# The first half of the down projection moved between the units of the up projection, as seven products throughout

## The chip, the cores and the metric

The kernel runs on one core of a Trainium2 chip. The metric is device time in microseconds (us) of one launch: the median of three runs before the change is 1566.11 us (1565.74 to 1566.63). The engines are named as the profile names them: PE (TensorE; its weight loads are PEld), DVE (VectorE), ACT (ScalarE), POOL (GpSimd) and SP (SyncE, which issues most DMAs).

## The reference

One block of a streaming encoder on 256 tokens, width 2048: a retention branch and a latent-attention branch are merged and added to the residual, and then comes the part that this case is about:

```python
h = h + mixer(rmsnorm(h))                      # all that comes before
z = rmsnorm(h, norm_mlp_g) @ w_up              # 256 x 2048 @ 2048 x 8192
h = h + square(relu(z)) @ w_down               # 256 x 8192 @ 8192 x 2048
return rmsnorm(h, norm_f_g)
```

Everything is float32. The row scale of the second rmsnorm is a positive number per token, so the kernel leaves it out of `z` and multiplies the down projection's result with its square (`rh2`).

## The kernel before

**Precision.** Each float32 operand is split in two fp32r parts: hi, a cast on ACT (`split`, L550), and lo, the difference, on DVE (L551). A product is then three matmuls: hi times hi, hi times lo, lo times hi.

**Three ways to multiply.** All take 256 tokens.
- A *unit* (`Unit`, L1239) makes 128 columns of `z`, transposed (columns on the partitions), with the weight as the stationary operand: 16 matmuls of 512 columns (L176: hi and lo of the tokens side by side) and 16 of 256 (L180), in two parts of 8 and 8, each with its own 512 KB load. Its result stands in one PSUM bank. `evict` (L1263) copies it on ACT (L1266), adds the two halves on DVE (L1267), and a little later Relu and Square on ACT and a store to DRAM (`hid`) follow.
- An *Eight* (`Eight`, L380) multiplies 256 rows by 1024 columns the plain way: a 2 by 2 product of blocks, 8 block products of 3 matmuls, 24 of 512 columns, in two parts. Tokens are the stationary operand. It sums in four banks, roles 0, 1, 4 and 7.
- A *seven-product step* (`Step` L287, `Seven` L417) does the same block product with 7 block products, 21 matmuls, in four parts of 6, 6, 6 and 3. It needs combinations of the weights, made on DVE (`prep`: fa at L307, fb at L316 and L317), and of the tokens (four mixed matrices), and seven banks, whose sums are combined at the end (`s_end` or `partial`). Its weight parts are 3.5 splits of 1024 columns.

**Up projection.** 8192 columns are 64 tiles of 128. The first 24 tiles are three blocks of 1024 columns, each 8 seven-product steps over the 2048 rows; the other 40 are units, set between the parts of the steps (after part 1 or part 3). The steps take mixed matrices of the normalised tokens, made by `hc.make` (L252). A step block's result has tokens on the partitions, so it is combined into `zo` (`s_end`, L515) and turned by 16 PE transposes per block (`turn`, L1277, L1284).

**Down projection.** `half` 0 gives the first 1024 output columns, half 1 the others; each runs over 32 pairs of hidden tiles. Half 0 has 10 Sevens and 22 Eights, half 1 12 Sevens and 20 Eights (`DS`). Each pair is loaded from `hid` and split again in both halves (`Hidden`, L1335); for a Seven its four mixed matrices are made once (`mix`, L1347, and `cut`), kept in `comb` and used again in half 1. The seven-products of a half are combined by `partial` (L444) some parts after its last Seven, into `gt[:, 1]`, and added to the residual `hn2` by `fold` (L1385) and `finish` (L1389). In half 0 the four roles stand in the pool `pmm` (4 banks) and the three other products in `pat` (4 banks); in half 1 it is the other way around (`Banks.add`, L349).

**Order.** The order of the work on each engine is written out by hand (`manual_schedule`): `stream` (L470) goes through a list of parts. Before a part's matmuls it issues the loads up to six parts ahead and the splits up to four parts ahead (`AHEAD`); after them come evictions, and then what stands in the list `later`, each entry after so many parts. Every engine's queue is in this order. Split parts stand in a ring of seven (`pair`), raw weights in five and two (`raw`, `sraw`). The residual (2 MB, POOL's queue) and `norm_f_g` (1 MB) are loaded at the first parts of half 0 (L1472 to L1476).

Of the kernel before, what the change touches and what calls it, by code (L numbers as in the profile page):

```python
# [30 lines left out]
SU = 3  # L31
SJ = KT // 2
ST = SU * 1024 // P
EARLY, LATE = 3, 2
AHEAD = 4
PAIRED = 6
MAKE = 7, 2 * EARLY + 18
SUMS = (4, 7, 10), (0, 1, 2)
# [7 lines left out]
DS = (4, 7, 9, 12, 14, 17, 19, 22, 24, 27), (3, 5, 7, 9, 11, 13, 15, 17, 19, 21, 24, 27)  # L46
# [59 lines left out]
def block_kernel(ctx: ExitStack, tc: tile.TileContext, A):  # L106
# [138 lines left out]
    class Combos:  # L245
        FORM = {2: 0, 5: 1, 6: 2, 4: 3}
        RAW = {1: (1, 0), 3: (0, 1), 7: (1, 1)}

        def __init__(self, name, pair):
            self.name, self.pair, self.t = name, pair, []  # L250

        def make(self, c):  # L252
            if c % 2 == 0:
                self.t.append(big(f"{self.name}{c // 2}", F32R, (P, KT // 4, 2, 4, P)))
            return combine(self.pair, 2 * c, self.t[-1][:, c % 2 * 2 : c % 2 * 2 + 2])

        def get(self, f, j):
            if f in self.RAW:
                k, t = self.RAW[f]
                ts = slice(t * P, (t + 1) * P)  # L260
                return self.pair.hi(2 * j + k, ts), self.pair.lo(2 * j + k, ts)
            o = self.t[j // 4][:, j % 4]
            return o[:, 0, self.FORM[f]], o[:, 1, self.FORM[f]]

# [22 lines left out]
    class Step:  # L287
        def __init__(self, qs, src, x, j, between, end):
            self.qs, self.src, self.x, self.j, self.between, self.end = qs, src, x, j, between, end
            self.ws = {}  # L290

        def load(self, part):
            if part:
                return
            self.rb = wtile("raw", [P, 2, 512])
# [9 lines left out]
        def prep(self, part):  # L305
            if part == 0:
                V.tensor_tensor(  # L307
                    out=self.fa, in0=self.rb[:, 1:].to_broadcast([P, 2, 512]), in1=self.ra, op=ALU.add
                )
                self.middle()  # L310
# [8 lines left out]
        def middle(self):  # L319
            pass  # L320

        def mm(self, part):
            if part == 0 and self.j == 0:
                self.qs.update({f: (mmps if f in (3, 4, 2, 5) else atps)(f"zs{uid[0]}{f}") for f in (3, 4, 2, 5, 6, 1, 7)})
            if part == 1:
                self.between()
# [90 lines left out]
    class Seven(Step):  # L417
# [4 lines left out]
        def load(self, part):  # L422
            if part == 0:
                self.h.load()
# [1166 lines left out]
```

## Time and profile before

| | |
|---|---|
| median of 3 runs | 1566.11 us (1565.74 to 1566.63) |
| span of the profiled execution | 1564.8 us |
| its own time beyond the span | not in the profile; the runs' median is 1.3 us above its span |
| PE busy | 1551.3 us (99%), 7655 matmuls |
| DVE busy | 1316.0 us (84%) |
| ACT busy | 962.6 us (62%) |
| POOL busy | 39.3 us (3%) |
| HBM | 319.72 MB read, 12.58 MB written, 212 GB/s over the span |

The page gives busy time per engine for the whole span; a window row gives the same for one stretch. In a timeline row stand the start in us from the span's first instruction, the duration, engine, line, operation, output<-inputs, shapes, and, in brackets, the idle time ahead of it with what ended it. A row with "x8" merges eight instructions. PE's matmuls overlap: the distance from start to start is what one costs, not the duration.

### The profile page before, as it was taken

How to read it: one execution, taken by the hardware profiler on the slowest of the kernel's cores; microseconds unless marked ns; L12 is line 12 of the kernel's file. 1: busy time of each engine (PE TensorE's matmuls, PEld its weight loads, DVE VectorE, ACT ScalarE, POOL GpSimd, SP SyncE). 2: the span in 40 equal slices, each digit the busy share in tenths (PEclk: the TensorE clock that was granted, in tenths of full speed). 3: DMA queues.
4: the chain of work that ended last, by engine and by line, in shares of the span. 5: the costliest groups of instructions: out<-in, count | busy, mean ns of one | idle time of the engine just before them, and what ended most of it. 6: DMA issues, size and time to landing. Idle time of an engine off the chain costs nothing.

```text
span 1564.8 us, 21391 instructions
## 1 busy us (share of the span) xinstructions
PE 1551.3 (99%) x7655; PEld 1311.0 (84%) x7655; DVE 1316.0 (84%) x1787; ACT 962.6 (62%) x1416; POOL 39.3 (3%) x76
## 2 busy tenths in 40 slices
PE   9999999999999999999999999999999999999997
PEld 7888888888898888888888888888888888888886
DVE  7898877799976988976567689887978899989996
ACT  6645655566545667875445567676767766656664
POOL 0000000000000000000000000000000100000000
PEclk9999999999999999999999999999999999999999
DMA  9666755566656654444556657666675977686873
GB/s 319 207 203 208 230 164 161 159 201 206 206 168 220 213 197 143 157 136 161 185 206 211 236 196 247 214 226 232 207 249 188 376 265 245 237 304 211 266 255 115
DMA packets 107626, 333.70 MB, mean 213 GB/s; under 512 B 11264, under 2 KB 12160, under 8 KB 106496
## 3 DMA queue, kind: packets, MB, share of 16 engines
q1 hardware_dynamic: 104208, 318.71, 61.1%
q0 software_dynamic: 3168, 11.54, 1.9%
q10 hardware_dynamic: 144, 2.10, 0.4%
q8 instruction: 60, 0.98, 0.3%
q14 instruction: 46, 0.38, 0.1%
HBM read 319.72 MB, written 12.58 MB: 212 GB/s over the span
## 4 chain that ended last, share of the span: by engine, by line
PE 79%; DVE 1%; issue 1%; ACT 1%; DVEq 0%; POOLq 0%; POOL 0%; ACTq 0%
PE z L176 9%; PE dn L358 7%; PE dn L359 7%; PE dn L357 7%; PE z L180 5%; PE zs L333 2%; PE zs L334 2%; PE zs L335 2%; PE mo L214 2%; PE mo L215 2%; PE mo L217 2%; PE wo L214 2%; PE wo L215 2%; PE wo L217 2%; PE gm L357 2%; PE yr L358 2%
## 5 line engine op out<-in xcount | busy, mean ns | idle before, releaser
L551 DVE TENSOR_TENSOR lo<-raw,hi 128x1024 fp32r<-128x1024 f32 (+3 forms) x214 | 232.0, 1101 | 22.7 <-ACT hi L550 22.2
L169 DVE TENSOR_TENSOR lo<-raw,hi 128x1024 fp32r<-128x1024 f32 (+1 forms) x148 | 173.2, 1171 | 89.7 <-ACT hi L168 89.6
L168 ACT CAST hi<-raw 128x1024 fp32r<-128x1024 f32 (+1 forms) x148 | 149.6, 1011 | 155.9 <-PE mo L215 44.9
L550 ACT CAST hi<-raw 128x1024 fp32r<-128x1024 f32 (+3 forms) x214 | 200.0, 953 | 55.3 <-issue 9.5
L551 DVE TENSOR_TENSOR morelo<-raw,morehi 128x1024 fp32r<-128x1024 f32 (+1 forms) x118 | 127.1, 1098 | 18.8 <-ACT morehi L550 18.3
L550 ACT CAST morehi<-raw 128x1024 fp32r<-128x1024 f32 (+1 forms) x118 | 109.1, 949 | 10.5 <-issue 3.2
L550 ACT CAST hi<-forms 128x1024 fp32r<-128x1024 f32 x70 | 73.7, 1052 | 51.2 <-DVE forms L307 28.1
L176 PE MATMUL z<-hT,morehi 128*128 128x512 f32 x408 | 101.6, 391 | 0.0
L357 PE MATMUL dn<-hi,dd 128*128 128x512 f32 x230 | 89.6, 389 | 0.0
L359 PE MATMUL dn<-hi,dd 128*128 128x512 f32 x230 | 89.5, 389 | 0.0
L358 PE MATMUL dn<-lo,dd 128*128 128x512 f32 x230 | 89.5, 389 | 0.0
L551 DVE TENSOR_TENSOR lo<-forms,hi 128x1024 fp32r<-128x1024 f32 x70 | 85.0, 1221 | 5.3 <-ACT hi L550 4.9
L176 PEld LDWEIGHTS z<-hT,morehi 128*128 128x128 f32 x408 | 74.9, 188 | 14.4
L1266 ACT COPY hs<-z 128x512 f32<-128x512 f32 x40 | 23.5, 587 | 71.2 <-PE z L180 71.1
L357 PE MATMUL dn<-morehi,dd 128*128 128x512 f32 x156 | 60.7, 389 | 0.0
L358 PE MATMUL dn<-morelo,dd 128*128 128x512 f32 x156 | 60.7, 389 | 0.0
L359 PE MATMUL dn<-morehi,dd 128*128 128x512 f32 x156 | 60.7, 389 | 0.0
L180 PEld LDWEIGHTS z<-hT,morelo 128*128 128x128 f32 x408 | 55.6, 190 | 4.0
L176 PE MATMUL z<-hT,hi 128*128 128x512 f32 x232 | 57.9, 392 | 0.0
L180 PE MATMUL z<-hT,morelo 128*128 128x256 f32 x408 | 56.9, 282 | 0.0
L307 DVE TENSOR_TENSOR forms<-raw,sraw 128x1024 f32<-128x1024 f32 x46 | 56.1, 1219 | 0.3 <-DMA raw<-w_up_s 0.3
L358 PEld LDWEIGHTS dn<-lo,dd 128*128 128x128 f32 x230 | 43.2, 188 | 9.0
(500 smaller groups left out, 4193.9 us busy)
## 6 DMA issues: line engine op xcount, KB each, us to landing
raw<-w_down SPq DMA_DIRECT2D x106, 512.0 KB, 6.0
raw<-w_up SPq DMA_DIRECT2D x80, 512.0 KB, 5.1
raw<-w_rv SPq DMA_DIRECT2D x32, 512.0 KB, 4.8
raw<-w_rg SPq DMA_DIRECT2D x32, 512.0 KB, 4.3
raw<-w_gret SPq DMA_DIRECT2D x32, 512.0 KB, 4.4
raw<-w_ret_o SPq DMA_DIRECT2D x32, 512.0 KB, 5.0
raw<-w_gmla SPq DMA_DIRECT2D x32, 512.0 KB, 4.3
raw<-w_mla_o SPq DMA_DIRECT2D x32, 512.0 KB, 3.7
```

The lines of the kernel that those rows point to most:

```text
L168: SC.copy(hi, raw)
L169: V.tensor_tensor(out=lo, in0=raw, in1=hi.bitcast(F32), op=ALU.subtract)
L176: PE.matmul(out, w[0][:, k], x.both(k0 + k), start=start and k == 0, stop=False)
L180: PE.matmul(out[:, :S], w[1][:, k], x.hi(k0 + k), start=False, stop=stop and k == n - 1)
L214: PE.matmul(out, x.hi(k0 + k, ts), w[0][:, k], start=start and k == 0, stop=False)
L215: PE.matmul(out, x.lo(k0 + k, ts), w[0][:, k], start=False, stop=False)
L217: PE.matmul(out, x.hi(k0 + k, ts), w[1][:, k], start=False, stop=stop and k == nk - 1)
L357: PE.matmul(q, ah, wh, start=start, stop=False)
L358: PE.matmul(q, ah, wl, start=False, stop=False)
L359: PE.matmul(q, al, wh, start=False, stop=self.left[f] == 0)
L550: SC.copy(hi, val)
L551: V.tensor_tensor(out=lo, in0=val, in1=hi.bitcast(F32), op=ALU.subtract)
```

## The change

- The up projection is 64 units. The three seven-product blocks, `Step`, `Combos`, `hc.make`, `s_end`, `turn` and the 48 transposes are gone. Units from the fourth on (`EARLY` = 3) take their bank from `pmm`, where three of four banks are held by half 0, so that one bank serves them all.
- Half 0 of the down projection is 32 Sevens, and none of it is an Eight. Its roles 1, 4 and 7 stand in `pmm`, products 2, 3, 5 and 6 in `pat`; role 0 isn't used. A step is cut into half-steps (parts 0 and 1, parts 2 and 3); after unit i comes half-step i - 5 (`LAG`), and the last five half-steps follow the last unit.
- Hidden tiles needn't be reloaded for it: after every second unit `Fresh.step` does Relu, Square and the store (step 0), the split and the mix (step 1), and the mixed matrices' split (step 2), one part apart. The twelve sets that half 1 needs are kept in `comb`.
- `partial` for half 0 is issued right after the last part, the folds 2 and 3 parts later, and finish and scale are moved back by 2 and 4 parts. The loads of `hn2` and `gt` are issued after half-step 58.
- Half 1 keeps its 12 Sevens and 20 Eights, with pairs in natural order; its loads of `hid` use the ring `hs` of 3 instead of one of 4.

```diff
-SU = 3
-SJ = KT // 2
-ST = SU * 1024 // P
-EARLY, LATE = 3, 2
+EARLY, LAG = 3, 5
...
     class Unit:
...
         def mm(self, part):
             if part == 0:
-                self.ps = atps(f"z{self.i}")
+                self.ps = (atps if self.i < EARLY else mmps)(f"z{self.i}")
...
         def evict(self):
-            pair, n = divmod(ST + self.i, 2)
-            t = zp.tile([P, 2, S], F32, tag="hs", bufs=5, name=f"hs{pair}{n}")
-            SC.copy(t, self.ps.rearrange("p (j n) -> p j n", j=2))
-            V.tensor_tensor(out=t[:, 0], in0=t[:, 0], in1=t[:, 1], op=ALU.add)
...
+            j, n = divmod(self.i, 2)
+            both = zp.tile([P, 2, S], F32, tag="zj", bufs=1, name=f"zj{self.i}")
+            SC.copy(both, self.ps.rearrange("p (j n) -> p j n", j=2))
+            if n == 0:
+                raws[j] = zp.tile([P, 2, S], F32, tag="hs", bufs=3, name=f"hs{j}")
+            V.tensor_tensor(out=raws[j][:, n], in0=both[:, 0], in1=both[:, 1], op=ALU.add)
+            if n:
+                later.extend([d + 1, lambda d=d: fresh[j].step(d)] for d in range(3))
...
+    class Fresh:
...
+        def step(self, d):
+            raw = raws.get(self.j)
+            if d == 0:
+                SC.activation(raw, raw, AF.Relu)
+                SC.activation(raw, raw, AF.Square)
+                G.dma_start(hid[self.j], raw)
+                self.t = hp.tile([P, 2, 2, S], F32R, tag="dd", bufs=4, name=f"dd{self.j}")
+                self.q = hp.tile([P, 4, P], F32, tag="dq", bufs=1, name=f"dq{self.j}")
+                if self.j in DS:
...
+                    self.c = sets[self.j] = combs[n // 4][:, n % 4]
+                else:
+                    self.c = hp.tile([P, 2, 4, P], F32R, tag="set", bufs=3, name=f"set{self.j}")
+            elif d == 1:
+                split(self.t[:, 0], self.t[:, 1], raw)
+                q, r = self.q, raw.rearrange("p k (t n) -> p (k t) n", t=2)
                 V.tensor_tensor(
                     out=q[:, :2], in0=r[:, :1].to_broadcast([P, 2, P]), in1=r[:, 1:3], op=ALU.subtract
                 )
                 V.tensor_tensor(out=q[:, 2], in0=q[:, 1], in1=r[:, 1], op=ALU.subtract)
                 V.tensor_tensor(out=q[:, 3], in0=q[:, 2], in1=r[:, 3], op=ALU.add)
+                raws.pop(self.j)
+            else:
+                split(self.c[:, 0], self.c[:, 1], self.q)
...
+    def end(banks):
+        sums = partial(banks, gt[:, 1].rearrange("p (i n) -> p i n", i=4))
...
+        d0 = 1 if banks.half else 0
+        later.extend([(d0 + 1) * d + d0, lambda: next(sums)] for d in range(2))
+        later.extend([2 * d + 5 if banks.half else d + 2, lambda d=d: spread(d)] for d in range(2))
+
+    both = [Banks("dn", 0, DP, DP), Banks("dn", 1, DP, len(DS))]
+    steps, fresh = [], [Fresh(j) for j in range(DP)]
+    for j in range(DP):
+        last = (lambda: end(both[0])) if j == DP - 1 else None
+        st = Seven(both[0], A["w_down"][0, j], fresh[j], j, last)
+        steps += [(j, st, (0, 1)), (j, st, (2, 3))]
+    early = [Unit(i) for i in range(EARLY)]
+    parts = [(e, h) for h in range(2) for e in early]
...
+    for i in range(EARLY, FT):
+        un = Unit(i)
+        parts += [(un, 0), (un, 1)]
+        if i >= LAG:
+            halfstep(i - LAG)
+    above = len(parts)
+    for n in range(FT - LAG, FT):
+        halfstep(n)
+    below = len(parts)
...
-        if hooks.get(n) == 0:
+        if n == above:
             hn2 = big("hn2", shape=(P, 2, D))
             G.dma_start(hn2, keep)
             gt = big("gt", shape=(P, 2, D))
             G.dma_start(gt[:, 0], A["norm_f_g"].partition_broadcast(P))
-        elif hooks.get(n) == 1:
+        elif n == below:
...
-                    later.append([2 * t + c, one])
-                    later.append([6 + 2 * t + c, lambda t=t, c=c: scale(t, c)])
+                    later.append([2 * t + c + 2, one])
+                    later.append([10 + 2 * t + c, lambda t=t, c=c: scale(t, c)])
```

291 lines of the change are left out of this document (70 added, 221 removed).

## The prediction

> **What bounds the kernel now.** I read first the page's busy shares, then the windows by stage, then TensorE's own order of work, and then VectorE's.
>
> ```profile
> PE 1551.3 (99%) x7655; PEld 1311.0 (84%) x7655; DVE 1316.0 (84%) x1787; ACT 962.6 (62%) x1416; POOL 39.3 (3%) x76
> ```
>
> ```profile
> 878.00:1222.00 344.00, 344.00 (x1839) 296.78 (x1838) 290.77 (x333) 235.75 (x337) 26.23 (x48) 1.00 0.66 225
> 1222.00:1390.00 168.00, 168.00 (x745) 139.14 (x744) 159.44 (x199) 109.36 (x141) 3.23 (x6) 1.00 0.81 289
> 1390.00:1551.00 161.00, 161.00 (x712) 133.32 (x711) 150.26 (x178) 98.72 (x129) 0.57 (x1) 1.00 0.65 219
> 1551.00:1565.00 14.00, 4.76 (x22) 3.60 (x20) 4.90 (x11) 4.30 (x10) 0.55 (x1) 0.81 0.40 150
> ```
>
> The rows are up projection, down half 0, down half 1 and the tail (length, then PE, PEld, DVE, ACT and POOL busy with counts, granted clock, DMA share, GB/s). TensorE is busy for all of the first three, so there the end moves with its issue time. VectorE is second: 290.8 of 344 us (85%), then 95%, then 93%. That is little reserve, and the change moves VectorE's work too.
>
> A busy PE need not be at its peak, so I time it from start to start. The boundaries of the stages on PE:
>
> ```profile
> 878.16 1.98 PE L176 MATMUL z<-hT,hi 128*128 128x512 f32 x8
> 1222.27 0.48 PE L357 MATMUL dn<-hi,dd 128*128 128x512 f32 x1
> 1389.68 0.39 PE L357 MATMUL dn<-hi,dd 128*128 128x512 f32 x1
> ```
>
> Up takes 1222.27-878.16 = 344.1 us; half 0, 738 matmuls (10 Sevens of 21, 22 Eights of 24), takes 167.4: 0.2268 each, although a row says 0.39. The chain of waits shows what a unit and a seven-product step cost among each other:
>
> ```profile
> 963.48 0.95 PE z L180 x8
> 969.22 1.81 PE z L176 x8
> ...
> 973.83 0.95 PE z L180 x8
> 977.53 1.81 PE z L176 x8
> ...
> 982.14 0.95 PE z L180 x8
> 985.16 1.81 PE z L176 x8
> ```
>
> A unit lasts 969.22 to 974.78, 5.56 us. Between units lie a whole step (964.43 to 969.22, 4.79), its parts 0 and 1 (974.78 to 977.53, 2.75) or parts 2 and 3 (983.09 to 985.16, 2.07).
>
> **TensorE's sum.** Before, up plus half 0: 344.1 + 167.4 = 511.5. After: 64 units at 5.56 = 355.8; the eight early transposes (L1199), which stay, 8 x 0.1 = 0.8 (estimated from the remainder of up: 344.1 - 40 x 5.56 - 24 x 4.79 = 6.7 us for 56 transposes and what follows them); half-steps 0 to 57 between units, 29 x (2.75 + 2.07) = 139.8; half-steps 58 to 63 in one run, 63 x 0.2268 = 14.3. Sum 510.7. So 24 units (+133.4) replace 24 steps (-115.0) and 48 transposes with their after-effects (-5.9), 66 matmuls of half 0 go (-15.0), and splitting steps costs 0.03 each time (+1.8 with the rounding). **Term 1: -0.8 us.** Half 1 has the same 732 matmuls.
>
> **VectorE's and ScalarE's work.** The pitch of VectorE's operations when it has a backlog (line, operation, tiles, shape):
>
> ```profile
> 1336.14 0.68 DVE L551 TENSOR_TENSOR dd<-hl,dd 128x512 fp32r<-128x512 f32 x1
> 1336.75 2.35 DVE L551 TENSOR_TENSOR lo<-raw,hi 128x1024 fp32r<-128x1024 f32 x2
> 1339.02 0.42 DVE L1356 TENSOR_TENSOR dq<-hl 128x256 f32<-128x256 f32 x1
> ...
> 1340.01 0.69 DVE L551 TENSOR_TENSOR dd<-hl,dd 128x512 fp32r<-128x512 f32 x1
> 1340.61 1.22 DVE L307 TENSOR_TENSOR forms<-raw,sraw 128x1024 f32<-128x1024 f32 x1
> 1341.74 0.69 DVE L551 TENSOR_TENSOR comb<-dq,comb 128x512 fp32r<-128x512 f32 x1
> 1342.34 1.22 DVE L551 TENSOR_TENSOR lo<-sraw,hi 128x1024 fp32r<-128x1024 f32 x1
> 1343.48 0.69 DVE L316 TENSOR_TENSOR forms<-forms,sraw 128x512 f32<-128x512 f32 x1
> ...
> 1344.81 1.22 DVE L551 TENSOR_TENSOR lo<-forms,hi 128x1024 fp32r<-128x1024 f32 x1
> ```
>
> So a split of 512 costs 0.605, of 1024 1.135, the mix (dq) 0.99, form fa 1.13, the two fb 1.33. A seven-product step is 1.13 + 3 x 1.135 + 1.33 + 0.605 = 6.47 us of VectorE against 21 x 0.2268 = 4.76 of TensorE. Alone it is VectorE-bound; a unit (2 x 1.135 and one addition) pays for it.
>
> What a unit's eviction does:
>
> ```profile
> 1081.67 0.40 PE L333 MATMUL zs<-morehi,hT 128*128 128x512 f32 x1
> 1081.87 0.59 ACT L1266 COPY hs<-z 128x512 f32<-128x512 f32 x1 [2.24 <-PE z L180]
> 1082.36 1.05 ACT L550 CAST hi<-forms 128x1024 fp32r<-128x1024 f32 x1
> 1082.49 0.43 DVE L1267 TENSOR_TENSOR hs<-hs 128x256 f32<-128x256 f32 x1
> ```
>
> ScalarE's copy waits for the unit's last matmul, and the next split (here of the part five places on: the preparation runs four parts ahead, AHEAD) stands behind it. So at every unit's end both engines are back in step with TensorE, and VectorE is free again 1.16 us after the unit (1082.49 + 0.34 - 1081.67). A lead larger than four parts isn't possible there.
>
> In the interleaved run a cycle is two units and two half-steps, 2 x 5.56 + 2.75 + 2.07 = 15.94 us of TensorE. VectorE has 4 x 1.135 + 2 x 0.34 + 6.47 + (0.605 + 0.99 + 0.605) for the pair of hidden tiles that Fresh splits and mixes = 13.9 us (87%). Walked through in program order, VectorE also idles behind ScalarE's Relu and Square, but is back 0.3 us ahead of the next copy, and each part is ready 3 us or more before its turn. The single bank of the units is emptied 0.8 us after a unit's end, under a half-step of 2.07 or more. **Term 2: 0**, covered by 0.3 us per cycle; without that cover each missing 0.1 us costs 29 x 0.1 = 2.9 us, once the 3 us of lead are used up.
>
> **The boundary of the halves.** After the last unit stand 5 half-steps with no unit between them (and half-step 58, prepared before). Zero is the end of unit 63. TensorE would want step 30's parts at 4.8, 6.1, 7.5 and 8.8, step 31's at 9.5, 10.9, 12.2 and 13.6, the first Eight of half 1 at 14.3. VectorE, in its order from 1.16: fa and part 0 3.4, fb 4.8, part 1 5.9; Fresh's split and mix of pair 31 (1.6) 7.5, part 2 8.6: wanted at 7.5 (a part's first matmul needs only hi, which gives 0.2), so 1.0 late. The set's split and part 3 9.8; step 31's part 0 12.1, late by 1.4 more; fb, part 1 14.6, 1.1 more; part 2 15.7, part 3 16.3; hidden split and first Eight 18.1. TensorE is there at 17.9 instead of 14.3. **Term 3a: +3.6.**
>
> There the second thing comes in. Half 1's first four products (roles 0, 1, 4, 7) go to the pool of four banks that half 0's products 3, 2, 5, 6 fill. Before, those were emptied four pairs ahead of the boundary:
>
> ```profile
> 1367.61 0.58 ACT L452 COPY gt<-dn 128x512 f32<-128x512 f32 x1
> 1369.88 1.41 DVE L448 TENSOR_TENSOR gt<-dn,gt 128x512 f32<-128x512 f32 x2
> 1371.21 1.22 DVE L551 TENSOR_TENSOR morelo<-raw,morehi 128x1024 fp32r<-128x1024 f32 x1
> ```
>
> Now the copies and the two additions (1.33) are issued after the last part of step 31, and thus behind the preparation of four more parts: the splits of the first two Eights, 18.1 + 1.135 + 1.74 + 1.135 = 22.1 on VectorE. ScalarE, which has fb at 13.4, still casts parts 2 and 3 of step 31 and the first two Eights (5 casts of 1024 at 0.95, the 1.05 of the cast row less its overlap, and 3 of 512 at 0.5), stands at 19.8 and ends its copies at 20.4 and 20.9 (0.58 each). Products 6 and 2 are released at 22.8 and 23.5. The first Eight then ends at 23.55 + 3 x 0.2268 = 24.25 instead of 17.0. **Term 3: +7.2 in all.** It would hardly be less if the banks were free: on VectorE there follow the four folds and the three finishing additions (0.67 each) and four scalings among Eights and Sevens, and step 7 of half 1 is ready only at 57.6 where an undelayed TensorE wants it at 51.0. Add 0.3 there for small waits. From below the term is 3.6 (banks free, VectorE catching up under Eights); from above 9.2, when the bank released last is the one the first product gets. I take 7.5, the walk's own end.
>
> The loads of the residual and of norm_f_g move to the same place:
>
> ```profile
> hn<-hnkeep POOLq DMA_DIRECT2D x1, 2048.0 KB, 10.8
> gt<-norm_f_g POOLq DMA_DIRECT2D x1, 1024.0 KB, 13.4
> ```
>
> Issued on POOL's queue behind pair 31's store, at about 4, they land at 15 and 18; the folds come after 25. Cost 0 under this cover; late landing would delay folds one to one. The 32 reloads of hidden pairs for half 0 fall away (8 MB) and take no time off a busy TensorE; making the four mixed matrices of hT (`hc.make`), which is dropped too, ran on VectorE beside a full TensorE: 0.
>
> **Sum.** 1564.8 - 0.8 + 0 + 7.5 = 1571.5 us span. The runs' median, 1566.11, is 1.3 above the profiled span: **1572.8 us**.
>
> The longest idle piece of that is 2.5 us (17.9 to 20.4). What a half clock costs is seen at the start:
>
> ```profile
> L573 PE MATMUL spin<-cold x8: 607/634/634, 1.2 to 4.2; 128*128 128x512 bf16 x8
> ```
>
> Eight matmuls fill 3.6 us (1.2 to 4.8); at 0.2268 they'd take 1.8. In the tail row above the granted clock falls to 0.81 only once PE stands still. The Trainium skill (TensorE: Matmul & The Clock Gate, Part 1, "What's actually happening") says that an idle window of about 3.4 us halves the clock and as long a busy one restores it. By it nothing is added at 2.5 us, and about 1.8 if the wait grows past 3.4; the tail agrees in kind, and no row shows a gap of that size mid-kernel.
>
> **The rivals.**
> 1. *Not slower: VectorE isn't in the written order.* If the planner puts the preparations of steps 30 and 31 ahead of unit 63's addition, VectorE enters the run with a lead. From 7.3 us of lead on, nothing is late: 1564.8 - 0.8 + 1.3 = 1565.3. For it: VectorE has 0.3 us spare in each cycle. Against: the eviction rows show the written order kept. Between, with half the lead, 1569.
> 2. *The wait is longer:* the last-released bank comes first (+1.9, 1574.7), and then the idle piece passes 3.4 us and the clock halves (+1.8, 1576.5).
> 3. *The units' stretch is VectorE-bound.* If Fresh's chain (addition, Relu, Square, splits) makes each cycle wait 0.5 us more than in my walk, VectorE misses 0.2 per cycle, 29 x 0.2 - 3.0 = +2.8 (1575.6); at 1.0 us more, +17 (1590). For it: 87% load in order; against: 85% was carried before without a gap.
>
> **How the numbers follow.** Forecast 0.62; rival 1 and its half case 0.14; rival 2 0.10; rival 3 0.14. What a measurement can tell is 0.2%, 3.1 us: below 1563.0 faster, above 1569.2 slower. Rival 1 gives 0.13 for no change and, if the shorter TensorE sum is undercounted by 2.5 us, 0.02 for faster; the rest is slower, 0.85. The range goes from just under the half case of rival 1, 1568, to the first case of rival 3 with the clock's loss, 1578.
>
> **What would show it.** In the changed profile: no PE gap between units; PE idle in the last 5 half-steps with the release by VectorE's lo; one longer PE idle at the first products of half 1, ended by the first of `partial`'s copies or additions; VectorE without idle time from the last unit to step 7. Wrong, if the boundary is gapless, or if the gaps are spread over the up stage.

## The result, and the profile after

The changed kernel takes 1574.59 us (median of 4 runs, 1574.33 to 1574.74) against 1565.92 us before (median of 4, 1565.62 to 1566.63): a ratio of 1.0053, 95% interval 1.0041 to 1.0065. It is slower by 8.7 us; the forecast was 1572.8, range 1568 to 1578. The profiled execution has a span of 1572.9 us (before 1564.8).

The page's busy shares have hardly moved, so the loss can't be read there:

```profile
PE 1553.4 (99%) x7805; PEld 1318.0 (84%) x7805; DVE 1319.8 (84%) x1835; ACT 965.9 (61%) x1400; POOL 28.4 (2%) x56
```

The windows by stage show the place. The rows are: first units; units with half-steps between them; the six half-steps behind the last unit and the wait behind those; the first 5 us of half 1; the rest of half 1; the end. Columns as in the prediction: length, then PE, PEld, DVE, ACT and POOL busy with counts, granted clock, DMA share, GB/s.

```profile
878.00:912.00 34.00, 34.00 (x198) 29.93 (x197) 25.18 (x40) 23.10 (x34) 1.27 (x2) 1.00 0.70 263
912.00:1374.00 462.00, 462.00 (x2467) 399.43 (x2466) 410.07 (x523) 311.38 (x407) 15.68 (x29) 1.00 0.65 213
1374.00:1395.00 21.00, 15.92 (x70) 11.97 (x68) 20.12 (x27) 15.13 (x20) 1.61 (x3) 1.00 0.93 351
1395.00:1400.00 5.00, 4.85 (x14) 3.85 (x15) 4.96 (x7) 4.58 (x7) 0.00 (x0) 0.66 1.00 379
1400.00:1562.00 162.00, 162.00 (x716) 134.03 (x716) 153.55 (x181) 96.58 (x129) 0.57 (x1) 1.00 0.68 228
```

TensorE (PE) is busy without a break in the units' stretch (462 of 462 us) and in the rest of half 1 (162 of 162). It stands still only in the third row, 15.92 of 21 us, where VectorE (DVE) is busy for 20.12 of 21; and in the fourth row the granted clock is 0.66. The rows of PE in that place, and its last matmul (start, duration, and in brackets the idle time ahead of it with what ended it):

```profile
1383.38 0.50 PE L325 MATMUL dn<-morelo,set 128*128 128x512 f32 x1 [0.92 <-DVE morelo L468]
1386.85 0.50 PE L325 MATMUL dn<-lo,dd 128*128 128x512 f32 x1 [1.14 <-DVE lo L468]
1389.32 0.50 PE L325 MATMUL dn<-lo,set 128*128 128x512 f32 x1 [0.81 <-DVE lo L468]
...
1392.40 0.39 PE L326 MATMUL dn<-hi,dd 128*128 128x512 f32 x1
1395.15 0.77 PE L324 MATMUL dn<-morehi,dd 128*128 128x512 f32 x1 [2.36 <-ACT gt L392]
1395.72 0.63 PE L325 MATMUL dn<-morelo,dd 128*128 128x512 f32 x1
...
1398.28 0.56 PE L325 MATMUL dn<-morelo,dd 128*128 128x512 f32 x1
1398.67 0.39 PE L326 MATMUL dn<-morehi,dd 128*128 128x512 f32 x1
...
1562.63 0.39 PE L326 MATMUL dn<-over,dd 128*128 128x512 f32 x1
```

Three parts of the last two seven-product steps come late, each at the matmul that needs the low half of a split (`lo`, `morelo`), for 0.8 to 1.1 us. Then the first product of half 1 waits 2.36 us for a bank, which ScalarE's (ACT's) first copy of the partial sums releases (L392). Then the next matmuls start 0.43 us apart instead of 0.227 (from 1395.72 to 1398.28 there are six such steps): the clock is halved. What the two engines do meanwhile, VectorE first, then ScalarE:

```profile
1375.44 0.43 DVE L1171 TENSOR_TENSOR hs<-zj 128x256 f32<-128x256 f32 x1 [0.71 <-ACT zj L1168]
1375.78 1.22 DVE L286 TENSOR_TENSOR forms<-raw,sraw 128x1024 f32<-128x1024 f32 x1
...
1384.44 1.22 DVE L286 TENSOR_TENSOR forms<-raw,sraw 128x1024 f32<-128x1024 f32 x1
...
1395.65 1.22 DVE L468 TENSOR_TENSOR lo<-raw,hi 128x1024 fp32r<-128x1024 f32 x1
1396.79 1.41 DVE L388 TENSOR_TENSOR gt<-dn,gt 128x512 f32<-128x512 f32 x2
```

```profile
1394.52 0.57 ACT L392 COPY gt<-dn 128x512 f32<-128x512 f32 x1
```

The written order is kept: the form `fa` of step 30 (L286) stands behind the addition of the last unit (L1171). From there VectorE has no bracketed idle time up to the partial sums at 1396.79, which stand behind all splits of the first two Eights, and the copies of ScalarE stand behind the casts for them.

The first matmul of the up projection, in PE's timeline after, and the last matmul of the down projection, in PE's timeline before:

```profile
878.12 1.98 PE L170 MATMUL z<-hT,hi 128*128 128x512 f32 x8
```

```profile
1555.37 0.39 PE L359 MATMUL dn<-over,dd 128*128 128x512 f32 x1
```

From the one to the other it is 1562.63 - 878.12 = 684.51 us after, and 1555.37 - 878.16 = 677.21 before. This distance, called **M** below, grew by 7.30 us. It holds all that the change moves and leaves out what precedes and follows.

### The profile page after: what moved, and what is told of

Same layout as the page of the kernel before. It is cut to its first block, busy times and chain, and to the rows that moved or that the text cites. A ratio compares the mean times of both kernels' runs of the same rounds, so it can differ in the third digit from the quotient of the medians.

```text
span 1572.9 us, 21634 instructions
## 1 busy us (share of the span) xinstructions
PE 1553.4 (99%) x7805; PEld 1318.0 (84%) x7805; DVE 1319.8 (84%) x1835; ACT 965.9 (61%) x1400; POOL 28.4 (2%) x56
## 4 chain that ended last, share of the span: by engine, by line
PE 78%; DVE 2%; ACT 1%; issue 1%; DVEq 0%; POOLq 0%; POOL 0%; ACTq 0%
PE z L170 15%; PE z L174 8%; PE dn L325 6%; PE dn L324 6%; PE dn L326 6%; PE mo L208 2%; PE mo L209 2%; PE mo L211 2%; PE wo L208 2%; PE wo L209 2%; PE wo L211 2%; PE gm L326 2%; PE yr L326 2%; PE yr L324 2%; PE gm L325 2%; PE gm L324 2%
## 5 line engine op out<-in xcount | busy, mean ns | idle before, releaser
L468 DVE TENSOR_TENSOR lo<-raw,hi 128x1024 fp32r<-128x1024 f32 (+3 forms) x235 | 257.2, 1107 | 33.9 <-ACT hi L467 33.4
L170 PE MATMUL z<-hT,hi 128*128 128x512 f32 x592 | 147.4, 391 | 0.0
L170 PEld LDWEIGHTS z<-hT,hi 128*128 128x128 f32 x592 | 108.6, 188 | 20.9
L468 DVE TENSOR_TENSOR morelo<-raw,morehi 128x1024 fp32r<-128x1024 f32 (+1 forms) x99 | 107.1, 1096 | 6.3 <-ACT morehi L467 6.3
L1168 ACT COPY zj<-z 128x512 f32<-128x512 f32 x64 | 37.6, 588 | 107.7 <-PE z L174 107.4
L174 PEld LDWEIGHTS z<-hT,lo 128*128 128x128 f32 x592 | 80.8, 190 | 5.8
L174 PE MATMUL z<-hT,lo 128*128 128x256 f32 x592 | 82.5, 282 | 0.0
L468 DVE TENSOR_TENSOR lo<-forms,hi 128x1024 fp32r<-128x1024 f32 x49 | 59.8, 1221 | 9.2 <-ACT hi L467 8.8
L325 PE MATMUL dn<-lo,dd 128*128 128x512 f32 x166 | 64.9, 391 | 1.1 <-DVE lo L468 1.1
L324 PE MATMUL dn<-hi,dd 128*128 128x512 f32 x166 | 64.8, 390 | 0.0
L326 PE MATMUL dn<-hi,dd 128*128 128x512 f32 x166 | 64.6, 389 | 0.0
L467 ACT CAST morehi<-forms 128x1024 fp32r<-128x1024 f32 x39 | 41.0, 1052 | 33.8 <-DVE forms L286 20.9
L286 DVE TENSOR_TENSOR forms<-raw,sraw 128x1024 f32<-128x1024 f32 x44 | 53.6, 1218 | 0.0
```

What stands on the lines that cost most here:

```text
L170: PE.matmul(out, w[0][:, k], x.both(k0 + k), start=start and k == 0, stop=False)
L174: PE.matmul(out[:, :S], w[1][:, k], x.hi(k0 + k), start=False, stop=stop and k == n - 1)
L324: PE.matmul(q, ah, wh, start=start, stop=False)
L325: PE.matmul(q, ah, wl, start=False, stop=False)
L326: PE.matmul(q, al, wh, start=False, stop=self.left[f] == 0)
L467: SC.copy(hi, val)
```

## The experiments

All twelve start from the changed kernel. M is worked out from the first and the last matmul as above; intervals are 95%. The edits shift line numbers by up to four (L326 of the changed kernel is L327 in some, L468 is L469 to L471).

| kernel | median us | ratio to before | M, us |
|---|---|---|---|
| changed kernel | 1574.59 | 1.0053 [1.0041, 1.0065] | 684.51 |
| x_fill | 1574.13 | 1.0053 [1.0038, 1.0068] | 684.50 |
| x_dose2 | 1580.58 | 1.0093 [1.0078, 1.0108] | 691.34 |
| x_sums | 1575.64 | 1.0062 [1.0047, 1.0077] | 685.74 |
| x_forms | 1572.07 | 1.0039 [1.0024, 1.0054] | 683.71 |
| x_loads | 1573.89 | 1.0053 [1.0038, 1.0068] | 684.40 |
| x_forms_loads | 1571.85 | 1.0039 [1.0025, 1.0053] | 682.96 |
| x_plain1 | 1571.91 | 1.0038 [1.0023, 1.0052] | 682.25 |
| x_plain1b | 1571.21 | 1.0033 [1.0020, 1.0046] | 681.51 |
| x_plain1c | 1571.33 | 1.0033 [1.0022, 1.0045] | 682.26 |
| x_plain2c | 1572.22 | 1.0042 [1.0025, 1.0059] | 682.89 |
| x_later | 1574.39 | 1.0053 [1.0038, 1.0068] | 684.18 |
| x_plain2d | 1566.47 | 1.0003 [0.9993, 1.0012] | 677.81 |

### The halved clock (x_fill)

Eleven matmuls into an unused bank keep TensorE busy while it would stand still at the first product of half 1.

```diff
+    def filled():
+        fill_end()
+        fill, t = mmps("fill"), fresh[DP - 1].t
+        for i in range(FILL):
+            PE.matmul(fill, t[:, 0, 0, :P], t[:, 0].rearrange("p j n -> p (j n)"), start=i == 0, stop=i == FILL - 1)
+
+    parts[below - 1][0].end = filled
```

> The changed kernel with 11 additional matmuls of 512 columns behind the last half-step, on operands that lie ready and into the bank that the units used; their result is used by nothing. They fill the 2.5 us in which TensorE stands still ahead of half 1 (11 x 0.227). Theory (the halved clock is set off by the standing still, and costs 1.7 us of its own): no matmul of half 1 at 0.43, the granted clock stays at 1.00, and the time falls by about 1.7 us, to 1572.9, although there is more work. Rival (the slow matmuls come from something else, the full DMA or the splits): they stay slow, time 1574.6 or a little more.

Measured: M 684.50, as without them; the theory's first half holds, the fall in time doesn't come. In the windows the clock now is 1.00 throughout, but another wait stands in the place of the slow matmuls. Window row and PE's row of this kernel:

```profile
1395.00:1400.00 5.00, 4.31 (x20) 3.08 (x19) 4.93 (x8) 3.07 (x4) 0.00 (x0) 1.00 0.91 280
```

```profile
1396.87 0.50 PE L325 MATMUL dn<-morehi,dd 128*128 128x512 f32 x1 [0.69 <-DVE gt L389]
```

So the halved clock costs this kernel nothing: at full speed TensorE reaches the next product at once and waits for the partial sums on VectorE (`gt`) until the same moment. The later kernel x_later shows the same without any added matmul: in its trace it keeps its clock and has the same M within 0.3 us. For the same reason one trace of x_fill can't show that the standing still halved the clock, since x_later stands still as long. The mean granted clock of all runs speaks for it: 0.998 in all four of x_fill, 0.997 in three of four of the changed kernel and of x_later; halving it for 3.4 us lowers the mean over 1573 us by 0.001.

### The reserve in the units' stretch (x_dose2)

Two more additions on VectorE (pitch 0.605 each by the prediction's rows) with every second unit from the seventh on, 1.21 us in a cycle of 15.94.

```diff
             V.tensor_tensor(out=raws[j][:, n], in0=both[:, 0], in1=both[:, 1], op=ALU.add)
+            if n == 0 and self.i > LAG:
+                for _ in range(2):
+                    V.tensor_tensor(out=both, in0=both, in1=both, op=ALU.add)
```

> The changed kernel with two more additions of 512 elements on VectorE (2 x 0.605 us) after the eviction of every even unit from the sixth on; they overwrite the unit's copy, which nobody reads any more, so the result is the same. It measures what spare time VectorE has per cycle of two units. By the walk through the order 0.25 us are idle ahead of the next addition and 0.36 more come back under ScalarE's cast: a dose of 1.21 costs 0.6 per cycle, and when 3 us of lead are gone, TensorE waits: 29 x 0.6 - 3 = +14 us, 1589. Rival (VectorE has as much room as its 89% say, 1.8 us per cycle): no change, 1574.6.

Measured: M +6.8 us and 1580.58 us, neither the theory's 1589 nor the rival's 1574.6. Of the 6.8, 4.4 arise up to the last unit and the rest at the boundary; its row for the units' stretch, to hold against the second row above:

```profile
912.00:1374.00 462.00, 462.00 (x2441) 392.33 (x2440) 434.68 (x573) 306.35 (x403) 15.69 (x29) 1.00 0.63 211
```

In the same 462 us 2441 matmuls start instead of 2467. The small waits come once per cycle and make it 16.15 us long, 0.21 more (the first at 1057, nine cycles in; until then the additions eat up the lead that the splits have). So of 1.21 us 1.0 was free. The reserve per cycle is about 1.0 us; the prediction had allowed 0.3.

### The partial sums first (x_sums)

All splits of half 1 but those of its first part wait until half 0's last part is done, so that copies and partial sums get ahead of them.

```diff
-            while prepped < min(len(parts), n + ahead + 1):
+            most = len(parts) if first is None or n >= first else first + 1
+            while prepped < min(most, n + ahead + 1):
...
-        stream(parts, after)
+        stream(parts, after, below)
```

> The changed kernel with half 0's last sums ahead of the preparations: until the last half-step is done, only the first part of half 1 is prepared, so that the copies and additions that release the four banks stand behind one split instead of four. The work is the same. Theory (VectorE's work in all, from the last unit to the seventh pair of half 1, sets the delay, and the banks only where it shows): no long wait at the first products, no halved clock (-1.7), but late parts in the first pairs of half 1, so that of the wait of 2.5 us only about 0.6 comes back: 1574.6 - 1.7 - 0.6 = 1572.3. Rival (the banks' wait is a cost of its own): it goes with the clock's loss, 1574.6 - 1.7 - 2.5 = 1570.4 or less.

Measured: M 685.74, 1.2 us longer; neither the theory's nor the rival's fall in time came. The banks are free in time, and the wait at the first product is gone; but three others come up in the first Seven of half 1, and behind them the clock is halved (steps of 0.43 us):

```profile
1411.39 0.50 PE L324 MATMUL dn<-morehi,comb 128*128 128x512 f32 x1 [1.19 <-ACT dn L1266]
...
1413.47 0.50 PE L324 MATMUL dn<-morehi,comb 128*128 128x512 f32 x1 [1.12 <-ACT dn L1266]
...
1415.03 0.50 PE L324 MATMUL dn<-morehi,comb 128*128 128x512 f32 x1 [0.60 <-ACT dn L1266]
...
1415.71 0.63 PE L326 MATMUL dn<-morehi,comb 128*128 128x512 f32 x1
...
1418.27 0.63 PE L326 MATMUL dn<-morehi,dd 128*128 128x512 f32 x1
```

There the three seven-products need the banks of half 0's roles, which are released by the squares (L1266) behind the finishing additions, and these are late because VectorE still has the same backlog. From start to start less 0.227 the three waits cost 3.4 us, where the one wait of the changed kernel cost 2.5, and the slow steps 1.7 us in both kernels. No wait follows the slow steps here, so no later wait takes them in; without them M would be about 684.0 (an estimate, 685.74 - 1.7; no run shows it), 0.5 less than in the changed kernel. The wait for the banks is thus in the main a consequence of the backlog: this order moves it and doesn't avoid it.

### Less work for VectorE (x_forms)

Steps 30 and 31 make no sums of their weights: `fa` and `fb` are left out (2 x 2.46 us of VectorE), and the splits read what stands in the buffers. This leaves out part of the computation, the combinations of the weights for the last two steps of half 0.

```diff
-                V.tensor_tensor(
-                    out=self.fa, in0=self.rb[:, 1:].to_broadcast([P, 2, 512]), in1=self.ra, op=ALU.add
-                )
+                if not self.old:
+                    V.tensor_tensor(
+                        out=self.fa, in0=self.rb[:, 1:].to_broadcast([P, 2, 512]), in1=self.ra, op=ALU.add
+                    )
...
-            if part == 0:
+            if part == 0 and not self.old:
```

> The changed kernel without VectorE's three combinations of weights (fa, fb) for the last two seven-product steps of half 0, which then use those of the two steps before them: 2 x 2.46 us of VectorE less in the stretch without units; the result isn't the reference's there. Loads, matmuls and banks are as they were. Theory (VectorE's load in this stretch makes the parts late): no late part in the last half-steps (3.7 us less), the wait at the first products of half 1 about 2.2 to 3 us, the clock's loss gone or 1.7: time 1568.9 to 1571.5. Rival (the loads of the residual and norm_f_g crowd the weights' loads out): 1574.6, with TensorE waiting in the same places. Rival (only the banks count): late parts go, the wait at half 1 grows by as much.

Measured: the late parts shrink from 3.7 to 0.6 us, as they should when VectorE causes them; M falls by only 0.8. The wait at half 1 has grown instead, and the clock is halved for twice as long. From the waits of PE, the windows from 1390 on, and ScalarE's timeline:

```profile
PE dn L327 <- ACT gt L395: 3.7, 1, 3.7
```

```profile
1390.00:1395.00 5.00, 1.86 (x4) 1.51 (x5) 4.37 (x6) 3.32 (x5) 0.00 (x0) 0.69 1.03 403
1395.00:1400.00 5.00, 5.00 (x16) 3.97 (x15) 4.96 (x8) 2.87 (x4) 0.00 (x0) 0.62 1.03 398
```

```profile
1391.56 1.04 ACT L470 CAST hi<-raw 128x1024 fp32r<-128x1024 f32 x1 [2.04 <-DMA raw<-w_down]
```

Of the 3.1 us won, the longer wait takes back 1.3 (3.9 us from start to start less one pitch, for 2.5) and the longer half clock 1.0 (slow steps of 2.7 us, for 1.7). The cast ahead of the copies waits for a load of `w_down`: a second limit seems to stand behind VectorE, the transfers. The runs below put that to the test.

### Loads that didn't move (x_loads, x_forms_loads)

Two of the three MB that GpSimd (POOL) loads at this place, the second half of `hn2` and `norm_f_g`, are written 8 parts into half 1, and the four scalings 16 parts later; once alone and once with the edit of x_forms (with the same part of the computation left out).

```diff
-            G.dma_start(hn2, keep)
+            G.dma_start(hn2[:, :, :1024], keep[:, :, :1024])
...
+        elif n == below + 8:
+            G.dma_start(hn2[:, :, 1024:], keep[:, :, 1024:])
             G.dma_start(gt[:, 0], A["norm_f_g"].partition_broadcast(P))
...
-                    later.append([10 + 2 * t + c, lambda t=t, c=c: scale(t, c)])
+                    later.append([26 + 2 * t + c, lambda t=t, c=c: scale(t, c)])
```

> The changed kernel with 2 of the 3 MB that POOL's queue loads at the end of the up projection (half of the residual, and norm_f_g) loaded eight parts into half 1, and the four scalings moved back by 16 parts. All else is as in the changed kernel. Theory (VectorE's order sets the waits there): the late parts and the wait for the banks stay, 1574.6, less 0 to 0.8 because four scalings leave the first pairs. Rival (the transfers crowd out the weights' loads): late parts or the long wait shrink by 2 us or more, 1572.5 or less.

> The kernel that leaves out the weight combinations of the last two steps of half 0, with the later loads too. Without the later loads ScalarE waited 2.0 us there for a load of w_down, and TensorE 3.9 us for ScalarE's copy, and the clock halved for 6.8 us. Theory (with VectorE relieved, the transfers are the next limit): ScalarE doesn't wait for the load, TensorE's wait falls to about 2, the clock halves for one window at most: 1572.1 - 2 to - 3.5 = 1568.6 to 1570.1. Rival (the order of the sums alone sets this wait): 1572.1 within 0.7.

Measured: M 684.40 and 682.96, 0.1 and 0.75 below their counterparts. The 0.75 is the clock's: in x_forms_loads it is halved for 3.4 us instead of 6.8, while TensorE's wait is no shorter (3.94 us of idle time for 3.70). This looks as if the transfers didn't matter. It doesn't show that, as GpSimd's timeline of x_loads tells:

```profile
1378.00 0.73 POOL L1347 DMA_DIRECT2D hn<-hnkeep  x1
1378.72 0.73 POOL L1350 DMA_DIRECT2D hn<-hnkeep  x1
1379.44 0.54 POOL L1351 DMA_DIRECT2D gt<-norm_f_g  x1
```

The third is issued at 1379.44; in the changed kernel it was at nearly the same time:

```profile
1378.91 0.54 POOL L1349 DMA_DIRECT2D gt<-norm_f_g  x1
```

GpSimd has nothing else to do there, so a later place in its program isn't a later time. The two runs say nothing of the transfers; x_later and x_plain2d below repeat the question.

### The last pair as an Eight (x_plain1, x_plain1b, x_plain1c)

The last pair of half 0 becomes a plain eight-product step, without mixed matrices: 3 matmuls more for TensorE (+0.7 us), two splits of 1024 (2.27 us) instead of 6.47 for VectorE, and the partial sums come one pair earlier. In x_plain1b the folds and finishing additions come earlier too; x_plain1c adds the edit of x_loads.

```diff
+PLAIN = 1
...
-    both = [Banks("dn", 0, DP, DP), Banks("dn", 1, DP, len(DS))]
+    both = [Banks("dn", 0, DP, DP - PLAIN), Banks("dn", 1, DP, len(DS))]
...
+        if j >= DP - PLAIN:
+            st = Eight(both[0], A["w_down"][0, j], fresh[j])
+            steps += [(j, st, (0,)), (j, st, (1,))]
+            continue
...
-        later.extend([2 * d + 5 if banks.half else d + 2, lambda d=d: spread(d)] for d in range(2))
+        later.extend([2 * d + 5 if banks.half else d + 3, lambda d=d: spread(d)] for d in range(2))
...
-                    later.append([2 * t + c + 2, one])
+                    later.append([2 * t + c, one])
```

(In x_plain1 the folds have `d + 6` for `d + 3`, and the last edit isn't there.)

> The changed kernel with the last pair of half 0 multiplied the plain way (an Eight: 24 matmuls instead of 21, 2.27 us of VectorE instead of 6.47, no mix for that pair), and the sums of the seven products issued after the pair before it. Theory: nothing is late in the last half-steps, the banks are empty before half 1 begins, the clock stays: 1574.6 - 7.9 + 3 x 0.227 = 1567.4, and TensorE without a gap from the up projection to the end. Rival (crowded loads): the gaps stay, 1575.3. Against the kernel before: +1.5 us, of which 0.9 lie in the last write, whose cause I don't know.

> The kernel with the last pair of half 0 multiplied the plain way, with the finishing additions two parts earlier (as they stood before the change) and the folds three parts earlier. In the version without this, TensorE waited 4.4 us in all for the squares on ScalarE that release the banks of roles 0, 1, 4 and 7, at the first seven-product step of half 1. Theory (this release is the next limit in the row, and it is late because finish and its square stand too far back in the order): these waits go, 1571.9 - 4.2 = 1567.7. Rival (VectorE's and ScalarE's load is the limit and the order doesn't matter): the waits move on by a pair or two, 1571 or more.

> The kernel with the last pair of half 0 as a plain eight-product step, folds and finishing additions earlier, and besides two of the three MB of hn2's and gt's loads, and the four scalings, put 8 and 16 parts later. Theory A: the 4.2 us that ScalarE stood waiting for a tile of w_down at 1390 were lost to the crowd of transfers there, so VectorE's idle 2.2 us behind it go, and with them most of the 4 to 5 us of small waits of half 1's first 40 us: first z matmul to last dn matmul 679 to 680 instead of 681.5, time 1568.5 to 1569.7. Theory B: the tile is late because its slot in the ring comes free late, or the next thing is late in its place: within 0.7 us of the kernel without the later loads, 1570.5 to 1572.

Measured: M 682.25, 681.51, 682.26. The late parts (but for 0.2 us) and the wait at half 1 are gone in all three, but instead of 7 us only 2 to 3 are won: x_plain1 misses its theory's 1567.4 by 4.5 us, x_plain1b comes out as its rival says and x_plain1c as its theory B. In x_plain1 the squares hold the banks, by PE's waits:

```profile
PE dn L325 <- ACT dn L1269: 3.3, 3, 2.1
```

In x_plain1b these are gone too, and splits are late again from 1407 to 1430. Their cause lies ahead, in VectorE's and ScalarE's rows:

```profile
1391.76 1.23 DVE L469 TENSOR_TENSOR morelo<-raw,morehi 128x1024 fp32r<-128x1024 f32 x1 [2.16 <-ACT morehi L468]
```

```profile
1390.67 1.05 ACT L468 CAST morehi<-raw 128x1024 fp32r<-128x1024 f32 x1 [4.21 <-DMA raw<-w_down]
```

VectorE, relieved, stands idle for 2.16 us at 1390, because the cast ahead of it waits 4.21 us for a load of `w_down`; what it loses there is missing at the first Sevens. In x_plain1c the wait for the load is still there, for the reason just seen, and the four moved scalings, which now stand between Sevens, cost a new wait of 1.2 us at 1455.

### Both limits (x_plain2c, x_later, x_plain2d)

x_plain2c makes the last two pairs Eights, with folds and finishing additions earlier as in x_plain1b, and has the loads and scalings of x_plain1c. x_later is the changed kernel with two of the three MB of loads truly later, on SyncE's (SP's) queue, where the loads of `w_down` ahead of them wait for free slots, and with the scalings, which need them, behind half 1's last Seven. x_plain2d is both: x_plain2c with these loads and scalings.

```diff
+PLAIN = 2
...
+        elif n == below + 46:
+            nc.sync.dma_start(hn2[:, :, 1024:], keep[:, :, 1024:])
+            nc.sync.dma_start(gt[:, 0], A["norm_f_g"].partition_broadcast(P))
...
-                    later.append([10 + 2 * t + c, lambda t=t, c=c: scale(t, c)])
+                    later.append([74 + 2 * t + c, lambda t=t, c=c: scale(t, c)])
```

(The first edit is in x_plain2c and x_plain2d, with the folds at `d + 5`; the others are in x_later and x_plain2d.)

> The last two pairs of half 0 as plain eight-product steps: TensorE gets 2 x 3 more matmuls than the changed kernel (+1.4 us), VectorE and ScalarE lose two seven-product preparations (6.5 us of VectorE each, against 2.3 for the plain one), and the partial sums are due two pairs before the boundary; loads and scalings later as in the kernel beside it. If the total of VectorE's work around the boundary sets the delay, nothing is late any more: first z to last dn matmul 677.2 - 0.7 + 1.4 = 677.9 to 678.5, time 1566.9 to 1567.7, the same as before. Rival: the work that is relieved uncovers another wait (squares holding banks, slots of the ring), and it stays at 680 or more, 1569.5 or more.

> The changed kernel with hn2's second MB and norm_f_g on SyncE's queue, 46 parts into half 1, behind loads of w_down whose slots hold them back; the four scalings after half 1's last seven-product step. (In the earlier kernel with later loads they stood on GpSimd's queue, which was free, and were issued at 1378 all the same.) Theory A: in the changed kernel the order of VectorE's work is the first limit, and the loads hide behind it: the three late parts, the wait of 2.5 us and the halved clock stay, 684.0 to 685.2 us from the first z matmul to the last dn matmul, 1573.5 to 1575. Theory B: the crowd of transfers from 1378 to 1402 has a share of its own: 683 us or less, 1572.5 or less.

> The kernel with the last two pairs of half 0 as plain eight-product steps, and the loads and scalings as in the kernel beside it. There VectorE had been relieved of 8 us and stood idle for 7 of them at 1388 to 1397, waiting for tiles of w_down that took 9 to 11 us to land while the DMA engines were full. If VectorE's work and the transfers are the two limits, one behind the other, nothing is late now: 677.2 - 0.7 + 1.4 = 677.9 to 678.7 us from the first z matmul to the last dn matmul, 1566.8 to 1568, no more than 0.2% from before. Rival: a third limit (folds, finishing additions and squares ahead of half 1's first seven-product step) keeps the waits of 1405 to 1414: 680 or more, 1569.5 or more.

Measured, x_plain2c: M 682.89, no better than one Eight, as the rival says. Its windows:

```profile
1385.00:1390.00 5.00, 5.00 (x24) 4.14 (x23) 3.38 (x5) 0.00 (x0) 0.00 (x0) 1.00 1.03 405
1390.00:1395.00 5.00, 5.00 (x24) 4.15 (x23) 2.00 (x2) 2.10 (x2) 0.00 (x0) 1.00 1.01 406
1395.00:1400.00 5.00, 5.00 (x24) 4.14 (x23) 3.35 (x5) 3.28 (x5) 0.00 (x0) 1.00 1.03 401
```

VectorE is busy for 8.7 of these 15 us, ScalarE for 5.4, and the DMA engines for all of them at 401 to 406 GB/s. From the DMA view of 1376 to 1400 (count, size, median us from issue to landing), and VectorE's and PE's rows further on:

```profile
raw<-w_down SPq DMA_DIRECT2D x9, 512.0 KB, 10.6
```

```profile
1449.81 0.68 DVE L1275 TENSOR_TENSOR hn<-hn,gt 128x512 f32<-128x512 f32 x1
...
1454.49 0.68 DVE L1275 TENSOR_TENSOR hn<-hn,gt 128x512 f32<-128x512 f32 x1
```

```profile
1410.17 0.50 PE L326 MATMUL dn<-lo,comb 128*128 128x512 f32 x1 [1.46 <-DVE lo L469]
...
1456.96 0.50 PE L326 MATMUL dn<-morelo,dd 128*128 128x512 f32 x1 [1.21 <-DVE morelo L469]
```

Two losses: late splits at 1406 to 1414 behind the idle time, and another at 1457 behind the four scalings (L1275), which the edit had put between half 1's Sevens. There VectorE has hardly any reserve: a Seven and an Eight with their hidden tiles cost it 6.47 + 0.605 + 2.27 + 0.605 = 9.95 us by the prediction's prices, and TensorE 45 x 0.2268 = 10.2.

x_later: M 684.18, against 684.51. The loads are issued 90 us later, by SyncE's timeline:

```profile
1468.80 0.62 SPq L1350 DMA_DIRECT2D hn<-hnkeep  x1
```

Its window row between 1385 and 1390 beside that of the changed kernel, the latter first:

```profile
1385.00:1390.00 5.00, 3.05 (x13) 1.89 (x12) 4.94 (x6) 2.83 (x4) 0.00 (x0) 1.00 0.98 410
```

```profile
1385.00:1390.00 5.00, 3.05 (x13) 1.89 (x12) 4.94 (x6) 3.03 (x4) 0.00 (x0) 1.00 0.50 166
```

Now the transfers have left (DMA share 0.50 for 0.98), and PE and VectorE do the same as before, to 0.01 us. In the changed kernel these loads are hidden, as theory A says.

x_plain2d: M 677.81, predicted 677.9 to 678.7; 1566.47 us, ratio 1.0003. Its window rows in the same place, and the load's line of the DMA view:

```profile
1390.00:1395.00 5.00, 5.00 (x24) 4.14 (x23) 4.78 (x7) 3.42 (x6) 0.00 (x0) 1.00 1.02 400
1395.00:1400.00 5.00, 5.00 (x24) 4.14 (x23) 5.00 (x7) 1.55 (x3) 0.00 (x0) 1.00 1.04 402
1400.00:1410.00 10.00, 10.00 (x46) 8.29 (x45) 9.96 (x13) 8.47 (x14) 0.00 (x0) 1.00 0.48 175
```

```profile
raw<-w_down SPq DMA_DIRECT2D x10, 512.0 KB, 8.0
```

TensorE has no wait between 1374 and 1440. With both 6.7 of the 7.3 us came back, with the transfers' relief alone (x_later) 0.3, in x_plain2c 1.6. But x_plain2c isn't VectorE's relief alone, since its moved scalings cost it time: of the 5.1 between x_plain2c and x_plain2d about 1.8 belong to them (the wait at 1457 with the slower matmuls around it), the rest, about 3.2, to the transfers. So VectorE's relief alone would have won about 3.4 (an estimate, 1.6 + 1.8; two Eights with loads and scalings unmoved weren't run; x_plain1b, one Eight with both unmoved, won 3.0). The remaining 0.6 over before is TensorE's own sum: -0.7 and the six added matmuls, +1.4.

What this settles: the boundary is limited by VectorE's backlog first, by the loads behind it (two of the 3 MB were moved), and by the squares' hold on the banks where the sums come earlier. One taken away shows the next. x_plain2d is as fast as the kernel before, not faster; no kernel here beats the one before.

## Why the prediction was right, point by point

- **What bounds the kernel, and Term 1 (-0.8): right.** The last half-0 matmul starts at 1392.40, so that half 1 could start at 1392.63, 514.51 after the first `z`; less the 3.7 us of late parts it is 510.8. The prediction's sum was 510.7.
- **Term 2 (0): right, its cover undersized.** No wait of PE between 912 and 1374. The reserve that it named, 0.3 us per cycle, is 1.0 by x_dose2. Rival 3 falls.
- **Term 3a (+3.6): right.** The three waits, from start to start less 0.227, are 1.08, 1.30 and 0.98, at the parts that the prediction named (predicted 1.0, 1.4, 1.1), and each is followed by a first matmul 0.1 longer: 3.7 in all. VectorE had no lead, as the row of the addition ahead of `fa` shows; rival 1 falls. x_forms shows that VectorE's work causes it: 3.7 becomes 0.6.
- **The rest of Term 3 (7.2 in all, taken as 7.5): right in place and releaser, its last piece in another form.** The wait for the first bank was 2.5 us (17.9 to 20.4); measured 2.52 from start to start less one pitch, released by the copy of L392. The 1.1 us for products 6 and 2 don't appear as a wait: the halved clock fills the same time, from 1395.15 to 1398.67 eight steps take 1.7 us more than 8 x 0.2268. Where the clock stays up, in x_fill and x_later, the predicted wait for `gt` is there, 0.69 and 0.70 us of idle time. In all 3.7 + 2.5 + 1.7 = 7.9, against 7.2 in the walk; the 0.3 allowed for small waits further on didn't come (162 of 162 us busy). M grew by 7.30; predicted -0.8 + 7.5 = 6.7.
- **"Hardly less if the banks were free": right.** With the banks free M was 1.2 us longer (x_sums), and would by estimate be 0.5 shorter if the clock had stayed up there.
- **The loads of the residual at 0: right here, for the reason given, and only under that cover.** x_later is the test, for two of the three MB. With VectorE's delay gone these cost about 3.2 us (x_plain2c against x_plain2d). The prediction looked only at when they land, not what they do to the loads of `w_down` beside them.
- **The clock gate: wrong, and by luck without effect.** "By it nothing is added at 2.5 us": the clock was halved after 2.4 us of idle time, from 1395.2 to 1398.6. It moved nothing, because VectorE is the later one (x_fill), and so it cost the forecast nothing; in x_forms, where no wait follows, the longer half clock costs 1.0 us. Rival 2 counted 1.8 us for it on top of the wait; that would have been wrong too.
- **The remaining 1.8 us** (1574.6 against 1572.8) are M (+0.6), the step from span to run, and the end. The prediction added 1.3 us to the span, the distance of the profiled span from the median of other executions; within one execution it is 1.7 to 1.8 for both kernels (+0.4). From the last matmul's start to the end of the span it is 1572.9 - 1562.63 = 10.3 us, before 1564.8 - 1555.37 = 9.4 (+0.9). In the other kernels here it is 9.2 to 10.3. The last operations of VectorE and ScalarE start 3.3 us after the last matmul in both, so the 0.9 lies in the last write; its cause stays open.

## What to carry to other kernels

A step that is bound by a second engine can be paid for by filler beside it, but where the filler ends the second engine's backlog comes due at once: let the last steps before such a boundary be of the kind that this engine does cheaply, and count what else (sums, bank releases, loads) is queued there behind it. Where taking away a wait wins little, look for the next one at the same place before giving up the theory: here VectorE's relief alone would have won about 3.4 us (estimate), the transfers' alone won 0.3, both 6.7. And after an edit that moves a transfer, look at its issue time: on a queue with nothing ahead of it a later place in the program is no later time.

## What the runs showed of the hardware

The clock fell to half after only 2.4 us of idle time, behind three waits of 0.8 to 1.1 us in the 11 us before it. It isn't a matter of the waits alone: x_later has the same four waits to 0.02 us, and its clock stays at 1.00. In PE's timeline of x_later:

```profile
1394.94 0.50 PE L324 MATMUL dn<-morehi,dd 128*128 128x512 f32 x1 [2.36 <-ACT gt L392]
1395.28 0.40 PE L325 MATMUL dn<-morelo,dd 128*128 128x512 f32 x1
```

The second matmul comes 0.34 us after the first and the next at 0.24, where the changed kernel has 0.57 and 0.43. Nor does it take one long gap: in x_sums the clock is halved from about 1415.5 on, behind idle times of 1.19, 1.12 and 0.60 us.

The alignment of the wait tells the changed kernel and x_later apart. In the changed kernel the clock falls at 1395.20 and again, at the end, at 1565.87: 170.67 us apart, 50 times the 3.413 us that the first halving lasted. Counted back by the same 50 from x_later's only fall after the start, at 1565.02, an edge lies at 1394.35 (an estimate). It cuts x_later's wait in two, 1.8 us and 0.6, while the changed kernel's wait lies whole in one stretch of 3.4 us, from 1391.79 to 1395.20.

The Trainium skill (TensorE: Matmul & The Clock Gate, Part 1, "What's actually happening") describes a window of about 3.4 us that runs freely and doesn't restart with the kernel; a halving that comes with one alignment and not with another agrees with that, and so do the 3.4 us that it lasted. But an idle window in its sense need not be idle throughout: in the one from 1391.79 on TensorE was at work until 1392.8, and in x_sums it worked between the waits. So the rule as the prediction read it, no halving below 3.4 us of standing still, doesn't hold here; the measurement decides.

In x_plain2c, at a DMA share of 1.0, the core's transfers stood at 401 to 406 GB/s, and a load of 512 KB took 10.6 us to land (median), against 8.0 with 2 MB less in the crowd (x_plain2d). The Trainium skill (DMA: Bandwidth & Descriptors, Specifications) gives 435 GB/s as the fabric's ceiling; these rows stay 7% below it.
